# Clip and store of the first tile in one piece instead of three, in a contrast kernel that streams 50 MB through one core

## The chip, the cores and the metric

The kernel runs on one core of a Trainium2 chip. The metric is the device time of one execution in microseconds. Before the change the median of three runs is 239.01 us, the lowest 238.9, the highest 239.16.

## The reference

The input holds 16 pictures of 3 channels, each channel 512 x 512 float32, so 48 images and 50.33 MB; the output has the same size. Each image is stretched around its own mean and clipped:

```
mean = np.mean(x, axis=(2, 3), keepdims=True)
return np.clip(mean + factor * (x - mean), 0, 1).astype(np.float32)
```

With factor f this is clip(f * x + (1 - f) * mean), so a shift per image and then one multiply-add and a clamp per element.

## The kernel before

The whole input is seen as rows of 8192 floats (32 KB, `ROW`), 32 rows to an image. A tile is 128 rows, one on each partition: 4 images, 4 MB. There are 12 tiles. They live in a ring of six slots in on-chip memory (`BUFS = 6`, 32 KB per partition and slot), and every tile is changed in place: it is loaded into its slot, summed, clipped and stored from the same slot.

Four helpers are defined in the kernel function. `load(t, n)` (line 82) issues a load of one tile, or of two in one DMA, from SyncE's queue (SP). `store(t, c0, c1)` (line 85) issues the store of columns c0 to c1 of a tile from ScalarE's queue. `add(t, c0)` makes the sums: ScalarE copies the tile onto itself and accumulates each row (line 96); for tile 0 alone the first 4352 columns are summed by VectorE (line 91) while ScalarE sums the other 3840. A matmul with a constant block matrix (line 100) then adds up the 32 rows of each image, scales by (1 - f) / 262144, and leaves the shift of every partition in PSUM; a float32 matmul is two instructions. `clip(t, c0, c1)` is two VectorE instructions over these columns: multiply by f and add the shift (line 104), then max with 0 and min with 1 (line 112).

The order on each queue is written out by hand. First the loads of tiles 0, 1, 2 and 3 together, and 4 and 5 together are issued. Tile 0 is summed. Then its clip and store are done piece by piece, with the borders given by the module constant `FIRST`:

```
for c0, c1 in zip((0, *FIRST), (*FIRST, ROW)):
    clip(0, c0, c1)
    store(0, c0, c1)
add(1)
```

With `FIRST = (1024, 3072)` the pieces have 1024, 2048 and 5120 columns; that is 4, 8 and 20 KB of each row, and each piece is a DMA of its own (0.5, 1 and 2.5 MB). After that a loop goes over tiles 1 to 11: clip of tile t, sum of tile t + 1, store of tile t (ahead of that sum for t = 1 and 3, behind it otherwise), and the load of tile t + 5. That load goes into the slot of tile t - 1, so SyncE waits before it until tile t - 1 has been stored; the first of these is the load of tile 6, which waits for the store of tile 0. On ScalarE's queue the issue of a store stands between the sums: while it waits for the clip, the sums behind it wait too.

Of the kernel before, what the change touches and what calls it, by code (L numbers as in the profile page):

```python
# [1 line left out]

# [4 lines left out]


P = 128  # L10
ROW = 8192
BUFS = 6
FIRST = (1024, 3072)


@with_exitstack
def kernel(
    ctx: ExitStack,
    tc: tile.TileContext,
    x: bass.AP,  # L20
    factor: float,
    out: bass.AP,
):

    nc = tc.nc
    f32 = mybir.dt.float32
    Alu = mybir.AluOpType
    Act = mybir.ActivationFunctionType  # L30

    B, C, H, W = x.shape
    n_img, n_pix = B * C, H * W
    ppi = n_pix // ROW
    per_tile = P // ppi
    n_tiles = n_img // per_tile
    assert ppi * ROW == n_pix and per_tile * n_tiles == n_img

    factor = float(factor)
    wconst = (1.0 - factor) / float(n_pix)  # L40

    x_f = x.rearrange("b c h w -> (b c h w)")
    out_f = out.rearrange("b c h w -> (b c h w)")

    def dram(ap, t, c0=0, c1=ROW, n=1):
        run = [[P * ROW, n]] if n > 1 else []
        return bass.AP(
            tensor=ap.tensor, offset=t * P * ROW + c0, ap=[[ROW, P], *run, [1, c1 - c0]]
        )

    consts = ctx.enter_context(tc.tile_pool(name="consts", bufs=1))
    xpool = ctx.enter_context(tc.tile_pool(name="xpool", bufs=1))
    small = ctx.enter_context(tc.tile_pool(name="small", bufs=1))
    psum = ctx.enter_context(tc.tile_pool(name="psum", bufs=1, space=bass.MemoryType.PSUM))


    sums = small.tile([P, 2 * n_tiles], f32, name="sums")
    bias = psum.tile([P, n_tiles], f32, name="bias")

    blockw = consts.tile([P, P], f32, name="blockw")  # L60
    blocks = blockw.rearrange("p (a b) -> p a b", b=ppi)
    nc.gpsimd.memset(blockw, wconst)  # L62
    for base, step in ((0, -ppi), (ppi - 1, ppi)):
        nc.gpsimd.affine_select(  # L64
            out=blocks,
            in_=blocks,
            compare_op=Alu.is_ge,
            fill=0.0,
            base=base,
            pattern=[[step, per_tile], [0, ppi]],  # L70
            channel_multiplier=1 if step < 0 else -1,
        )


    ring = xpool.tile([P, BUFS, ROW], f32, name="ring")

    def slots(t, n=1, c0=0, c1=ROW):
        k = t % BUFS
        return ring[:, k, c0:c1] if n == 1 else ring[:, k : k + n, :]

    def load(t, n=1):
        nc.sync.dma_start(out=slots(t, n), in_=dram(x_f, t, n=n))  # L82

    def store(t, c0=0, c1=ROW):
        nc.scalar.dma_start(out=dram(out_f, t, c0, c1), in_=slots(t, 1, c0, c1))  # L85

    def add(t, c0=0):
        own = sums[:, 2 * t : 2 * t + 2]
        parts = []
        if c0:  # L90
            nc.vector.tensor_reduce(  # L91
                out=own[:, 0:1], in_=slots(t, 1, 0, c0), axis=mybir.AxisListType.X, op=Alu.add
            )
            parts.append(own[:, 0:1])
        part = slots(t, 1, c0)
        nc.scalar.activation(out=part, in_=part, func=Act.Copy, accum_out=own[:, 1:2])  # L96
        parts.insert(0, own[:, 1:2])
        shift = bias[:, t : t + 1]
        for k, part in enumerate(parts):
            nc.tensor.matmul(shift, blockw, part, start=k == 0, stop=k == len(parts) - 1)  # L100

    def clip(t, c0=0, c1=ROW):
        part = slots(t, 1, c0, c1)
        nc.vector.tensor_scalar(  # L104
            out=part,
            in0=part,
            scalar1=factor,
            scalar2=bias[:, t : t + 1],
            op0=Alu.mult,
            op1=Alu.add,  # L110
        )
        nc.vector.tensor_scalar(  # L112
            out=part, in0=part, scalar1=0.0, scalar2=1.0, op0=Alu.max, op1=Alu.min
        )

    with tc.manual_schedule():
        load(0)
        load(1)
        load(2, 2)
        load(4, 2)  # L120
        add(0, 4352)
# [4 lines that stand above are left out]
        for t in range(1, n_tiles):  # L126
            clip(t)
            if t in (1, 3):
                store(t)
            if t + 1 < n_tiles:  # L130
                add(t + 1)
            if t not in (1, 3):
                store(t)
            if t + BUFS - 1 < n_tiles:
                load(t + BUFS - 1)


# [1 line left out]
_INS = ['x', 'factor']  # L139
_OUTS = [((16, 3, 512, 512), 'float32')]  # L140

_NUMBERS = {'factor': 1.5}


# [26 lines left out]
```

## Time and profile before

| what | us |
|---|---|
| median of three runs | 239.01 |
| profiled execution, its own time | 238.72 |
| span of the profiled execution | 237.0 |
| VectorE busy | 112.1 |
| ScalarE busy | 82.9 |
| one tile's clip, its two VectorE instructions | 4.49 and 4.43 |
| one tile's sum on ScalarE | 7.03 |

The span goes from the first to the last instruction; some 1.7 us of the profiled execution lie around it. The profile's second part cuts the span in 40 slices and gives the busy share of every engine in tenths, and of the 16 DMA engines together. A stretch of time can be asked for by its ends; its row gives length, then busy time and instructions of TensorE's matmuls and weight loads, VectorE, ScalarE and GpSimd, then TensorE's granted clock, the DMA engines' share, and GB/s. In the timeline a row is start, length, engine, line, operation, tiles; ACTq is the DMA issuing of ScalarE's queue, SPq that of SyncE's. Issuing is merged over neighbouring instructions ("x3" with the time from the first to the end of the last). The packet records of the trace have one entry for each piece that a DMA engine moved: here one row of a tile, and a 4-byte packet with which a DMA reports its end.

### The profile page before, as it was taken

To read this page: it belongs to the slowest core of one execution; us is meant where nothing else is said; L and a number is where in the kernel's file an instruction comes from. 1 tells how busy PE (TensorE), PEld (TensorE's weight loads), DVE (VectorE), ACT (ScalarE), POOL (GpSimd) and SP (SyncE) were. 2 spreads that over 40 slices of the span, in tenths; PEclk is the share of its full clock that TensorE was granted. 3 is DMA by queue.
4 is the path that set the end of the run, shared out by engine and by line. 5 is a ranking of instruction groups with operands and counts; after the bars stand their busy time and mean duration, and the time that the engine had idled before them with its cause. 6 is when DMAs were issued, how large, how long until landed. Compare 5 with 4: busy or idle time off the path is not lost.

```text
span 237.0 us, 211 instructions
## 1 busy us (share of the span) xinstructions
PE 7.6 (3%) x26; PEld 6.5 (3%) x26; DVE 112.1 (47%) x29; ACT 82.9 (35%) x25; POOL 1.0 (0%) x7
## 2 busy tenths in 40 slices
PE   0000000000000000000000000000000000000000
PEld 0000000000000000000000000000000000000000
DVE  0078708609990059979209407704902920950000
ACT  2050190299100894650380091083056029000000
POOL 1000000000000000000000000000000000000000
DMA  7999998999999999999999999999999999999996
GB/s 265 442 442 442 398 459 383 441 428 435 465 426 404 409 442 442 442 442 442 442 426 431 404 420 442 442 442 442 442 442 426 415 398 442 442 442 442 442 442 265
DMA packets 3712, 100.66 MB, mean 425 GB/s; under 512 B 384, under 2 KB 384, under 8 KB 512
## 3 DMA queue, kind: packets, MB, share of 16 engines
q1 hardware_dynamic: 1696, 50.33, 49.6%
q10 hardware_dynamic: 2016, 50.33, 49.2%
HBM read 50.33 MB, written 50.33 MB: 425 GB/s over the span
## 4 chain that ended last, share of the span: by engine, by line
DMA 39%; DVE 25%; another core or an unknown queue 11%; ACT 9%; issue 3%; PE 1%; ACTq 1%; SPq 0%
DMA out_dram<-ring 20%; DMA ring<-in_x_dram 18%; DVE ring L104 11%; DVE ring L112 11%; ACT ring L96 9%; DVE sums L91 2%; PE bias L100 1%; ACTq L85 1%; SPq L82 0%
## 5 line engine op out<-in xcount | busy, mean ns | idle before, releaser
L96 ACT ACTIVATE ring<-ring 128x8192 f32<-128x8192 f32 (+1 forms) x12 | 80.7, 6724 | 117.3 <-DMA ring<-in_x_dram 95.3
L104 DVE TENSOR_SCALAR ring<-ring,bias 128x8192 f32<-128x8192 f32 (+3 forms) x14 | 54.3, 3880 | 84.9 <-PE bias L100 84.9
L112 DVE TENSOR_SCALAR ring<-ring 128x8192 f32<-128x8192 f32 (+3 forms) x14 | 53.4, 3817 | 0.5
L100 PE MATMUL bias<-sums,blockw 128*128 128x1 f32 x26 | 7.6, 361 | 194.0 <-ACT ring L96 193.5
L100 PEld LDWEIGHTS bias<-sums,blockw 128*128 128x128 f32 x26 | 6.5, 312 | 195.0 <-ACT ring L96 177.7
L91 DVE TENSOR_REDUCE sums<-ring 128x1 f32<-128x4352 f32 x1 | 4.7, 4685 | 13.1 <-DMA ring<-in_x_dram 13.1
L96 ACT ACTIVATION_READ_ACCUMULATOR ring<-ring 128x1 f32 x12 | 2.2, 186 | 0.0
L96 ACT ACT_TABLE_LOAD x1 | 1.3, 1283 | 0.8 <-PEq L152 0.8
L64 POOL TENSOR_SCALAR_AFFINE_SELECT blockw<-blockw 128x128 f32<-128x128 f32 x2 | 0.6, 311 | 0.1
L62 POOL MEMSET blockw<- 128x128 f32 x1 | 0.2, 204 | 0.3 <-POOLq L152 0.3
L152 POOL MEMSET const-uint8-127<- 128x1 uint8 x1 | 0.1, 103 | 0.0
L152 POOL MEMSET const-bfloat16-1.0<- 128x1 bf16 x1 | 0.1, 102 | 0.0
L152 POOL MEMSET const-float32-0.0<- 128x1 f32 x1 | 0.1, 98 | 0.3 <-issue 0.3
L152 POOL MEMSET const-float32-1.0<- 128x1 f32 x1 | 0.1, 98 | 0.0
## 6 DMA issues: line engine op xcount, KB each, us to landing
out_dram<-ring ACTq DMA_DIRECT2D x11, 4096.0 KB, 48.5
ring<-in_x_dram SPq DMA_DIRECT2D x8, 4096.0 KB, 31.4
ring<-in_x_dram SPq DMA_DIRECT2D x2, 8192.0 KB, 59.5
out_dram<-ring ACTq DMA_DIRECT2D x1, 2560.0 KB, 37.3
out_dram<-ring ACTq DMA_DIRECT2D x1, 1024.0 KB, 25.8
out_dram<-ring ACTq DMA_DIRECT2D x1, 512.0 KB, 16.1
```

The source lines that it names most:

```text
L62: nc.gpsimd.memset(blockw, wconst)
L64: nc.gpsimd.affine_select(out=blocks, in_=blocks, compare_op=Alu.is_ge, fill=0.0, base=base, pattern=[[step, per_tile], [0, ppi]], channel ...
L85: nc.scalar.dma_start(out=dram(out_f, t, c0, c1), in_=slots(t, 1, c0, c1))
L91: nc.vector.tensor_reduce(out=own[:, 0:1], in_=slots(t, 1, 0, c0), axis=mybir.AxisListType.X, op=Alu.add)
L96: nc.scalar.activation(out=part, in_=part, func=Act.Copy, accum_out=own[:, 1:2])
L100: nc.tensor.matmul(shift, blockw, part, start=k == 0, stop=k == len(parts) - 1)
L104: nc.vector.tensor_scalar(out=part, in0=part, scalar1=factor, scalar2=bias[:, t : t + 1], op0=Alu.mult, op1=Alu.add,)
L112: nc.vector.tensor_scalar(out=part, in0=part, scalar1=0.0, scalar2=1.0, op0=Alu.max, op1=Alu.min)
L152: nc = _bacc.Bacc("TRN2", target_bir_lowering=False, num_devices=1)
```

## The change

The constant that holds the borders is empty. The loop over pieces then runs once, with columns 0 to 8192: tile 0 is clipped by one pair of VectorE instructions over 8192 columns and stored by one DMA of 128 rows of 32 KB, as all other tiles are. Nothing else differs.

```
 ROW = 8192
 BUFS = 6
-FIRST = (1024, 3072)
+FIRST = ()
```

## The prediction

> **What bounds the kernel now.** First the page, parts 1 to 3, for which resource is full; then stretches of time cut at landings, for whether that resource runs at one rate; then the timeline of ScalarE's queue, for when stores are issued; last the trace's records of single DMA packets, for what stands on each of the 16 DMA engines in what order (the records give start, length, size and queue of each packet; from them I only take times).
>
> ```profile
> span 237.0 us, 211 instructions
> PE 7.6 (3%) x26; PEld 6.5 (3%) x26; DVE 112.1 (47%) x29; ACT 82.9 (35%) x25; POOL 1.0 (0%) x7
> DMA  7999998999999999999999999999999999999996
> DMA packets 3712, 100.66 MB, mean 425 GB/s; under 512 B 384, under 2 KB 384, under 8 KB 512
> q1 hardware_dynamic: 1696, 50.33, 49.6%
> q10 hardware_dynamic: 2016, 50.33, 49.2%
> ...
> 12.75:22.43 9.68, 1.15 (x4) 1.00 (x4) 8.57 (x6) 3.50 (x2) 0.00 (x0) 1.00 1.00 433
> 35.77:47.95 12.18, 0.56 (x2) 0.47 (x2) 8.92 (x2) 2.22 (x1) 0.00 (x0) 1.00 1.01 430
> 47.95:65.15 17.20, 1.17 (x4) 1.00 (x4) 11.59 (x3) 11.92 (x4) 0.00 (x0) 1.00 1.00 425
> 84.56:181.38 96.82, 3.52 (x12) 3.01 (x12) 53.42 (x12) 42.65 (x13) 0.00 (x0) 1.00 1.00 434
> ...
> 20.00 8.52 ACTq L85 DMA_DIRECT2D out_dram<-ring  x3
> 28.56 7.03 ACT L96 ACTIVATE ring<-ring 128x8192 f32<-128x8192 f32 x1 [11.96 <-DVE ring L112]
> ...
> 193.87 7.03 ACT L96 ACTIVATE ring<-ring 128x8192 f32<-128x8192 f32 x1 [12.25 <-DMA ring<-in_x_dram]
> 193.93 0.34 ACTq L85 DMA_DIRECT2D out_dram<-ring  x1
> 200.80 0.19 ACT L96 ACTIVATION_READ_ACCUMULATOR ring<-ring 128x1 f32 x1
> 210.65 0.34 ACTq L85 DMA_DIRECT2D out_dram<-ring  x1
> ```
>
> VectorE is at 47%, ScalarE at 35%; the DMA digits are 9 from the second slice to the last but one, and the two queues (q1 loads, q10 stores) together fill 98.8% of the 16 engines' span. The last two columns of a stretch are DMA share and GB/s: pure loads run at 433, loads beside stores of 32 KB rows at 434, and only the two stretches in which the 8 KB and the 20 KB rows of tile 0 are stored are below, at 430 and 425. By the packet records every engine works without a gap from 1.81 (the first engine; 2.45 the last) to 235.83 us. One 32 KB packet takes 1.213 us, and a tile's 8 packets per engine pass in 9.68 us: pure loads land at 12.75 and 22.43, the last stores at 197.11 and 235.83, 4 tiles in 38.72 us. While both queues have work, an engine takes one packet of each in turn, whatever the sizes, and the 9 ns packet that ends a DMA is a turn too. So the end is 24 tiles of packets, plus what is lost to gaps and slow packets; when a store is issued matters only if an engine runs dry.
>
> **The change, part by part.** The sum is made against the profiled execution: 238.72 us, span 237.0, 1.72 around it. It lies 0.29 under the median 239.01 of the runs shown (238.9 to 239.16); I carry the difference over to the median.
>
> VectorE: the six clips of tile 0 (758, 694, 1284, 1226, 2883, 2827 ns, together 9.67 us) become two of 8192 elements (4.49 + 4.43 = 8.92). Clipping starts at 18.48 as before and ends at about 27.45, not 28.10. This is cover only: the DMA engines have loads queued for 6 tiles, 58 us, so it costs and brings nothing.
>
> ScalarE's queue: three issues (20.00, about 22.4, 28.18) become one at 27.45. Behind it the sum of tile 1 starts near 27.8 instead of 28.56, and tile 1's store is issued near 44.6 instead of 45.35. Nothing else stands between on that queue, and SP and POOL aren't passed by anything. If the work on chip were the limit, the gain would be 0.7 us, and the later first store a loss of up to 7.45 us; with the engines full both are 0.
>
> The Trainium skill, DMA: Bandwidth & Descriptors, section Rules for kernel authors, advises to issue a DMA early, so that its setup overlaps compute. The change does the reverse for the first 4 KB of each row; what that would make is the rival of the delay, below, and the gapless packets speak against it here.
>
> DMA work: 256 extra packets go from the store queue, 16 per engine, and two closing packets of 9 ns on each engine. By length the three small rows take 0.159 + 0.309 + 0.761 = 1.229 us against 1.213, times 8 rows per engine 0.13 us. Beside this some 49 loads among the small rows between 35 and 65 us took 1.25 to 1.52 us, on some engines and not on others; among the 32 KB stores from 67 to 236 us none did. What both cost the engine that ends last follows from its landings: 12.75 us for tile 0, then 23 tiles at 9.68 give 235.39, against 235.83 in the trace. So 0.44 us of the span is owed to the small pieces. I take all of it as gained, since the new order of packets is that of 67 to 236 us; at the least the shorter packets alone, 0.06 to 0.13 us, or nothing if the slow loads have another cause. The other end of this term is a loss: if the first 32 KB stores beside loads ran like the stretch of 425 GB/s for two tiles (38.7 us at 2% less), 0.8 us.
>
> When the stores start: the first store now was issued at 20.00 and its first packets started at 24.21 on the first engine, behind three loads, 4.2 us later. Issued at 27.45 it should start at about 31.5, behind 24 loads (1.81 + 24 x 1.21, with the first packet longer by 0.8). Tile 0 then lands at about 51 instead of 65.15, since its large rows take equal turns, and load 6, which waits for it on SP, is issued near 51 instead of 65.57; its queue is full until about 88, so that earlier issue brings nothing. Tiles 2 and 3 land near 51 instead of 44.91 and tiles 4 and 5 near 89 instead of 77.3, as stores take half of the turns; loads end near 204.7 instead of 193.48.
>
> What is late next: a load's landing to the issue of its store takes 193.48 to 210.65, 17.17 us (0.39 to ScalarE, 7.03 + 0.19 sum, 0.6 matmul, 8.92 clip). At the end 25 store packets per engine are left (now 35), 17 of them ahead of the last tile's: 17 x 1.21 = 20.6 us. The engines' stagger of 0.63 us taken off, the last store may need 20.6 - 17.17 - 0.63 = 2.8 us from issue to first packet before an engine runs dry; now it is some 15. The nearest rows for this need are the first load, issued at 0.80, with first packets at 1.81 to 2.45 (1.0 to 1.65), and the first store, 4.2, which stood behind loads already committed. At the end no load is there, so I take 1.0 to 1.65 and cost the edit at 0; with 4.2 the gap would be 1.4 us. The stores of tiles 2 and 4 have similar or more slack, and a late one there costs nothing: a load takes the turn, and that leaves one more store packet, 1.21 us more slack each, for the end.
>
> Sum: 237.0 - 0.44 = 236.56 span, 238.28 with the 1.72, and 239.01 - 0.44 = 238.57, say 238.6, on the median's scale.
>
> **The rivals.**
>
> Slow loads stay: they belong to that time (ScalarE and VectorE both at work in 47.95 to 65.15) and not to the sizes. For it: they fell on only some engines. Against it: 84.56 to 181.38 has the same work beside it at 434. Gain 0.06 to 0.13: 238.9.
>
> The last store comes late (slower): the last tile's path of 17.17 us becomes the end. It decides from a need above 2.8 us between issue and first packet; at the 4.2 of the first store the gap is 1.4, the time 239.01 - 0.44 + 1.4 = 240.0. Against it stands that the same need would first delay the store of tile 2, which has the same 2.8 us, and so add slack.
>
> Large rows hurt the early loads (slower): the 0.8 us above, in place of the gain: up to 239.8. The stretch at 434 speaks against it.
>
> The delay passes through (slower): if the store stream set the end, its later start, 27.45 for 20.00, would move the end by 7.45, to 246.5. Against it: from 24 to 193 us the engines split their turns between both queues without a gap, and loads fill what stores leave.
>
> Each DMA has a fixed price on the engines: the first load was issued at 0.80 and landed at 12.75, 2.27 us more than its 9.68. Two DMAs fewer would then give 4.5 us, 234.5. Against it: four stores end to end took 38.72, just 4 x 9.68, so that price overlaps.
>
> The Trainium skill, same page, section Anatomy of one DMA, puts the fixed part at about 2 us for DMAs issued from GpSimd, mostly the wait for the write's receipt; by it two DMAs fewer would be an estimated 4 us.
>
> **How the numbers follow.** Forecast 0.65; slow loads stay 0.18; late last store 0.09; delay passes through 0.01; large rows hurt 0.05; fixed price 0.02. What can be told from no change is 0.2%, 0.48 us: the border is 238.53, just past the forecast's 238.57, so its 0.65 is split, 0.32 faster and 0.33 same, for the median moves by 0.1 between runs. Adding 0.02 to the first and 0.18 to the second: faster 0.34, same 0.51, slower 0.15. The forecast's own range is 238.2 to 238.9. The whole range goes from 238.1 to 239.4: it takes in the slow loads, a part of the gap and of the hurt, and leaves out the fixed price, the 4.2 us case and the worst of the large rows.
>
> **What would show it.** Packets: 3712 - 256 - 32 = 3424, under 8 KB 352. One ScalarE-queue issue near 27.4. Stretches of 433 to 434 GB/s from 12.75 to the end, no load over 1.25 us after the first. Load 6 issued near 51, loads ending near 204.7, the last store issued near 222 and its packets directly behind those before. Tile 0 landing at 65 would show the turns wrong; a drop in the last slices' DMA digits, a store that came late; a span of 237.0 with all this in place, that slow loads were not the small rows'.

## The result and the profile after

The changed kernel takes 243.03 us, median of six runs (241.21 to 243.27), against 238.95 for the kernel before (238.9 to 239.16). The ratio, of the means, is 1.0157, with a 95% interval of 1.0127 to 1.0186: slower, where the forecast was 238.6 and the range ended at 239.4. The profiled execution took 242.78, with a span of 241.1 us.

The page of the changed kernel, parts 1 to 3:

```profile
span 241.1 us, 200 instructions
PE 7.6 (3%) x26; PEld 6.5 (3%) x26; DVE 111.5 (46%) x25; ACT 82.9 (34%) x25; POOL 1.0 (0%) x7
DMA  7999999999999999999999999999999999999993
DMA packets 3424, 100.66 MB, mean 418 GB/s; under 512 B 352, under 2 KB 352, under 8 KB 352
q1 hardware_dynamic: 1696, 50.33, 49.8%
q10 hardware_dynamic: 1728, 50.33, 48.4%
```

The work is what was forecast: 3424 packets, 352 of them small, and VectorE has 0.6 us less to do. The DMA digits still read 9 from the second slice on, so the engines are no less occupied; only the last digit is 3 in place of 6. The same bytes at 418 GB/s in place of 425 are the loss. The busy share hardly shows it, since packets that take longer count as busy.

Stretches of the changed kernel, about a tile's loads and stores each but for the longer second one (last column GB/s):

```profile
32.50:51.80 19.30, 0.58 (x2) 0.50 (x2) 8.92 (x2) 2.60 (x2) 0.00 (x0) 1.00 1.00 433
52.50:88.20 35.70, 1.18 (x4) 1.01 (x4) 17.75 (x4) 14.13 (x4) 0.00 (x0) 1.00 1.00 432
109.00:128.50 19.50, 0.59 (x2) 0.50 (x2) 15.91 (x4) 7.12 (x2) 0.00 (x0) 1.00 0.99 418
128.50:148.00 19.50, 0.59 (x2) 0.50 (x2) 8.92 (x2) 7.12 (x2) 0.00 (x0) 1.00 0.99 418
148.00:167.50 19.50, 0.58 (x2) 0.50 (x2) 8.92 (x2) 7.12 (x2) 0.00 (x0) 1.00 1.01 425
167.50:187.00 19.50, 0.59 (x2) 0.50 (x2) 8.48 (x2) 7.12 (x2) 0.00 (x0) 1.00 1.00 425
```

The kernel before has these for the same stage:

```profile
103.93:123.29 19.36, 0.58 (x2) 0.50 (x2) 8.92 (x2) 7.11 (x3) 0.00 (x0) 1.00 1.00 433
123.29:142.65 19.36, 0.59 (x2) 0.50 (x2) 8.92 (x2) 7.13 (x3) 0.00 (x0) 1.00 1.00 432
142.65:162.01 19.36, 0.59 (x2) 0.50 (x2) 8.92 (x2) 7.11 (x3) 0.00 (x0) 1.00 1.00 433
```

So the early stage, in which the change was made, runs at 432 to 433 from the first store row on, and most of the loss lies 60 to 150 us later, where both kernels issue the same instructions with the same row sizes. Its place is seen in the packet records. Before, not one 32 KB packet that starts between 90 and 200 us takes over 1.25 us. After, 128 do: 115 loads and 13 stores. They stand at the seam of two tiles, one or more at a seam. This is one DMA engine of the changed kernel at two seams (start, length in us, queue, bytes):

```
109.24 0.009 load 4         129.26 0.009 load 4
109.25 1.321 store 32768    129.26 1.213 store 32768
110.56 1.213 load 32768     130.47 1.213 load 32768
111.77 0.009 store 4        131.68 0.009 store 4
111.78 1.589 load 32768     131.69 2.089 load 32768
113.36 1.213 store 32768    133.78 1.220 store 32768
114.57 1.378 load 32768     134.99 1.213 load 32768
```

A load DMA ends (the 4-byte packet), one store row later the store DMA of the tile three before it ends, and the next load row takes 1.59 or 2.09 us in place of 1.213. In all, 44 of the 115 slow loads come right behind the packet that ends a store DMA and 53 are the second load behind it; each of the 13 slow stores, as the one at 109.25, comes right behind the packet that ends a load DMA. One engine of the kernel before at such a seam, with three store rows between the two ends:

```
115.71 0.009 load 4
115.72 1.213 store 32768
116.93 1.213 load 32768
118.14 1.213 store 32768
119.35 1.213 load 32768
120.56 1.213 store 32768
121.76 1.213 load 32768
122.97 0.009 store 4
122.98 1.213 load 32768
```

Per engine the slow packets of this stage add up to 0.73 to 3.53 us, 1.98 on average. Since the engines differ, they fall apart: the last load ends between 206.35 and 209.51 us (before 193.13 to 193.48), and the last store between 237.3 and 239.76 (before 235.48 to 235.84).

At the end, the timeline of ScalarE's queue after:

```profile
209.89 7.03 ACT L96 ACTIVATE ring<-ring 128x8192 f32<-128x8192 f32 x1 [12.39 <-DMA ring<-in_x_dram]
209.95 0.34 ACTq L85 DMA_DIRECT2D out_dram<-ring  x1
216.83 0.19 ACT L96 ACTIVATION_READ_ACCUMULATOR ring<-ring 128x1 f32 x1
226.67 0.34 ACTq L85 DMA_DIRECT2D out_dram<-ring  x1
```

The sum of the last tile starts when the slowest engine has landed its load, and the store follows 16.78 us later, as before. The fastest engines finish the store ahead of it at 226.93 and stand idle until 227.52, 0.6 us. The slowest finishes it at 230.08 and goes straight on to 239.76. So the idle time is a result of the spread and doesn't set the end.

### The profile page after: what moved, and what is told of

The parts are those of the page before. It is cut to its first block, busy times and chain, and to the rows that moved or that the text cites. A ratio compares the mean times of both kernels' runs of the same rounds, so it can differ in the third digit from the quotient of the medians.

```text
span 241.1 us, 200 instructions
## 1 busy us (share of the span) xinstructions
PE 7.6 (3%) x26; PEld 6.5 (3%) x26; DVE 111.5 (46%) x25; ACT 82.9 (34%) x25; POOL 1.0 (0%) x7
## 2 busy tenths in 40 slices
DMA packets 3424, 100.66 MB, mean 418 GB/s; under 512 B 352, under 2 KB 352, under 8 KB 352
## 4 chain that ended last, share of the span: by engine, by line
another core or an unknown queue 36%; DVE 24%; issue 14%; ACT 12%; DMA 5%; PE 1%; ACTq 1%; DVEq 0%
ACT ring L96 12%; DVE ring L104 11%; DVE ring L112 11%; DMA ring<-in_x_dram 5%; DVE sums L91 2%; PE bias L100 1%; ACTq L85 1%; DVEq L104 0%
## 5 line engine op out<-in xcount | busy, mean ns | idle before, releaser
L104 DVE TENSOR_SCALAR ring<-ring,bias 128x8192 f32<-128x8192 f32 x12 | 53.9, 4490 | 101.6 <-PE bias L100 101.6
L112 DVE TENSOR_SCALAR ring<-ring 128x8192 f32<-128x8192 f32 x12 | 53.1, 4426 | 0.4
```

The lines of the kernel that those rows point to most:

```text
L104: nc.vector.tensor_scalar(out=part, in0=part, scalar1=factor, scalar2=bias[:, t : t + 1], op0=Alu.mult, op1=Alu.add,)
L112: nc.vector.tensor_scalar(out=part, in0=part, scalar1=0.0, scalar2=1.0, op0=Alu.max, op1=Alu.min)
```

## The experiments

What a run has to tell is by how many rows the loads lead the stores. A number that can be read off each engine is N, the store rows that are left when its last load has ended; N modulo 8 (called r here) is how many store rows stand between the end of a load DMA and the end of the next store DMA; on an engine it stays the same from tile to tile. Each trace holds one execution, so N and the slow packets are those of that one; its time is given as "traced" where it lies off the median, and what the others lost isn't shown. Unless said otherwise, slow packets "after 90 us" are counted up to 200 us. Before, N is 35 on all engines, r = 3; after, 25 on 14 engines and 26 on two, r = 1 and 2.

Three theories were set against each other: the phase (r decides), the large first rows (32 KB rows into an empty store queue disturb the engines for good), and the distance (three tiles between loads and stores are too few). Delays were made by clamping values again that are clamped already, ahead of the first store.

**One piece, 3.0 us later.**

```
clip(0, 0, 8192)
again(5440)          # max 0, min 1 over columns 0 to 5440
store(0, 0, 8192)
```

> One piece, and VectorE clamps the first 5440 columns of tile 0 a second time before its store is issued (about 3.0 us, values unchanged). The store stream starts about 3 rows later: when the loads end, 27 to 28 store rows are left instead of 25. Theory of the phase (loads are slow where a load DMA and a store DMA end within a row or two of each other on an engine; now they are three rows apart, as before the change): the slow loads at every tile from 92 to 195 us go, the 0.9 us at the first store stays, 239.5 to 240.2 us. Theory of the large first rows (the first store of 32 KB rows sets the engines apart and that goes on): 242.5 to 243.5. Theory of the distance (stores three tiles behind the loads disturb them, four tiles don't): 242.5 to 243.5. If only the delay counted: 246.

Measured: 240.57 us (239.85 to 241.01; traced 239.85), ratio 1.0068 [1.0051, 1.0085]; N is 27 on 13 engines and 26 on three. One packet after 90 us is slow instead of 128. A delay took 2.5 us off the time. The large first rows are out as the cause of the late loss, and so is the distance of about three tiles. The median lies a little above the range of the phase.

**One piece, 8.9 us later**: `again(8192)` twice.

> One piece, and VectorE clamps the whole of tile 0 twice more before its store is issued (about 8.9 us, values unchanged). The store stream starts 7 to 8 rows later: 32 to 33 store rows are left when the loads end, so DMA ends fall together as after the change, at four tiles' distance. Theory of the phase: slow loads at every tile as after the change, 242 to 243.5 us. Theory of the large first rows: 242.5 to 243.5. Theory of the distance: 239.5 to 240.

Measured: 239.62 us, ratio 1.0028 [1.0019, 1.0038], no slow packet after 90 us. The expectation had put the bad phase at r = 0; N came out as 31 on 15 engines and 32 on one, and neither is bad. The time fits the distance, which the run before had ruled out. So the theory of the phase as it was written here failed, and what was left was that r = 1, perhaps 2, is the bad phase.

**Two pieces**: `FIRST = (1024,)`.

> Two pieces, of 1024 and 7168 columns (rows of 4 and 28 KB). The first store starts as before the change, so 27 store rows are left when the loads end. Theory of the phase: three rows apart, no slow loads per tile, 238.4 to 239.2 us. Theory of the large first rows: as before the change, 238.8 to 239.3, if 4 KB first is what protects. Theory of the distance: three tiles' distance, 242 to 243.

Measured: 239.24 us, ratio 1.0016 [1.0002, 1.003]; N is 27 on 12 engines and 26 on four, no slow packet after 90 us. It rules out the distance once more. It lies just above the phase's range and inside that of the large first rows, so it doesn't tell these two apart.

**The kernel before with its first store 7.1 us later**: `again(1024)` ten times after the first piece.

> The kernel before, with ten further clamps of the first 1024 columns (about 7.1 us, values unchanged) ahead of the first store. The store stream starts 6 rows later: about 41 store rows are left when the loads end instead of 35, DMA ends within a row of each other, at five tiles' distance. Theory of the phase: slow loads at every tile, 241 to 243 us though the first rows are small. Theory of the large first rows, and of the distance: as before, 238.8 to 239.3.

Measured: 239.25 us (238.84 to 240.57, four of ten above 240; traced 238.98), ratio 1.0021 [1.0003, 1.004], no slow packet after 90 us. It told nothing apart: N was 37 and not 41, since the load queue ran empty for a few rows, waiting for the store of tile 0. The bad phase was not reached.

**All stores ahead of the sums, in the changed kernel.** This tests a further theory, that the slow loads come from a store being issued just at the seam.

```
-            if t in (1, 3):
+            if True:
                 store(t)
             if t + 1 < n_tiles:
                 add(t + 1)
-            if t not in (1, 3):
+            if False:
                 store(t)
```

> The changed kernel with every store issued ahead of the next tile's sum, so at the end of its clip and not when the next load has landed (in the changed kernel's trace the stores of tiles 6 to 10 are issued at 130.3, 150.4, 170.7, 190.4 and 209.95, just as the engines pass from one tile to the next). The order of packets stays, 25 rows are left at the end of the loads. Theory of the issue (slow loads come from a store being issued while the engines are at the seam of two tiles): no slow loads after 92 us, 239.5 to 240. Theory of the phase (load DMAs and store DMAs end within a row or two of each other): 242.5 to 243.3 as without this edit.

Measured: 242.74 us, ratio 1.0155 [1.0138, 1.0172], 126 slow packets after 90 us. When the store is issued doesn't matter.

**One piece, 10.7 us later**: `again(8192)` twice and `again(3072)`.

> One piece, and about 10.7 us of further clamps of tile 0 ahead of its store (values unchanged). About 33 rows are left when the loads end: the same phase as after the change, one row after the load's end, but eight rows further back. Theory of the phase: slow loads at each tile, 241.5 to 243.5. Theory of the distance (the stores are too close behind the loads, about three tiles): no slow loads at the tiles, 239.4 to 240.

Measured: 242.28 us, ratio 1.0139 [1.0122, 1.0156]; N is 33 on 15 engines, r = 1. The ratio is of three executions, 242.18 to 242.32. The traced one was far longer (251.55 us) because of a single engine that no longer agrees with the others: with N = 32 it had 11.7 us of slow packets after 90 us and ended at 248.55, the others by 237.7. On those others the slow packets came to 0.46 to 1.6 us. Eight rows more of distance and the same r give about the same time as after the change, as the phase had it, and 1.8 us less delay (the run with 8.9) takes the loss away.

**Tiles 2 to 5 loaded one by one, in the changed kernel.** Each 4-byte packet that ends a DMA is a turn of its queue, so two more load DMAs let the stores catch up.

```
-        load(2, 2)
-        load(4, 2)
+        load(2)
+        load(3)
+        load(4)
+        load(5)
```

> The changed kernel with tiles 2, 3, 4 and 5 loaded by a DMA each. Two more packets that end a load take a turn, so stores gain one row: 24 left instead of 25, and load and store DMAs end in neighbouring turns. Tile 2 also lands 5 to 10 us earlier, so its store is early. Theory of the phase: slow loads at the tiles as after the change or worse, 242 to 244. Theory of the distance: the same. Theory of the issue: 242 to 243. If 24 rows are free of it, it is the one row between the ends that matters, 239.5 to 240.

Measured: 239.78 us, ratio 1.0033 [1.0023, 1.0044]; N is 23 on 13 engines and 24 on three. No slow packet after 90 us but a few store rows at the very end. With no delay, and one or two rows nearer than the changed kernel, the slowdown is gone, against the expectation of the phase as it was written here (242 to 244). On three engines the packet that ends a store DMA follows directly behind the one that ends a load DMA; on 13 the store DMA ends one load row and one store row ahead of the load DMA, the mirror image of the changed kernel. So two ends close together do no harm by themselves.

**One piece, 1.8 us later**: `again(3136)`.

> One piece, and about 1.8 us of further clamps ahead of the store of tile 0. About 26 rows are left. In the run with 3.0 us, four engines with 26 rows left had no slow loads at the tiles. Theory of the phase on each engine by itself: 239.5 to 240.5, no slow loads. Theory of a resource that the engines share, where most of them must be in the bad phase: with most engines at 26, either none, 239.5 to 240.5, or about as after the change, 242 to 243, if two rows are still too near.

Measured: 242.07 us (240.76 to 242.19), ratio 1.0119 [1.0093, 1.0146]. The 11 engines at N = 26 have 0.08 us of slow packets after 90 us on average, the five at 25 have 1.09 (0.5 to 2.65). One of these ended at 239.19 and set the time; the others ended by 237.5. So within one run the engines part by their r, and one engine is enough to make a run slow. But each engine by itself isn't the whole of it: the two engines of the changed kernel at r = 2 (N = 26), beside 14 at r = 1, lost 2.7 and 2.8 us, and those at r = 2 here next to nothing. This trace also has 26 slow loads between 60 and 90 us, 0.5 us per engine, most of them at 72 to 76 where the store of tile 2, issued at 69.31, comes in; the changed kernel has none between 60 and 90. (The run with 3.0 us had three engines at 26, not four.)

**The crossing: the kernel before, with tiles 2 to 5 loaded one by one.** The edit to the loads is the one shown above for the changed kernel, on the other kernel.

> The kernel before, three pieces, with tiles 2 to 5 loaded by a DMA each. Two more packets that end a load take a turn after the first store has started, so the stores gain two rows on the loads: 33 left when the loads end instead of 35, one row after the end of a load DMA. Theory of the phase (slow loads where a store DMA ends one or two rows after a load DMA): slow loads at each tile, 241.5 to 243 us, though the three pieces are kept and nothing else is changed. Theory of the pieces (the small first rows are what protects): 238.8 to 239.3.

Measured: 250.76 us (248.91 to 252.5; traced 252.5), ratio 1.0491 [1.043, 1.0552]. r is 1 on 15 engines and 0 on one, and 141 packets after 90 us are slow. The page of this kernel:

```profile
span 250.8 us, 212 instructions
DMA  7999999999999999999999999999999999997900
```

The two zeros at the end are one engine at work and 15 that have finished: 15 ended by 238.8 us, and one at 249.44, the one with r = 0. On that engine 37 of the 45 store rows between 73 and 195 us took 1.29 to 1.86 us, anywhere in a tile, and only two of the 45 loads were slow. That is not the picture of slow loads at the seams, and the theory of the phase doesn't hold it: it expected 241.5 to 243, about what the other 15 engines would give (238.8 and the 3.1 us that lay between the last store's end and the time in the kernel before, 241.9). The edit that took 3.3 us from the changed kernel adds 11.8 to the one before, some 10 of them by this one engine.

**The same edit with two pieces.**

> Two pieces of 1024 and 7168 columns, with tiles 2 to 5 loaded by a DMA each. 25 rows left instead of 27, the phase of the changed kernel. Theory of the phase: 241.5 to 243.5 us, against 239.24 for the two pieces with the paired loads. Theory of the pieces: 239 to 239.5.

Measured: 243.05, 251.32, 251.79 and 254.24 us, too far apart for a ratio; the profiled execution is the shortest, with N = 25 on all engines as far as their packets can be followed, 133 slow packets after 90 us, and a span of 241.3. That one lies in the range of the phase; the others, at least 8 us longer, have no trace. Two pieces alone took 239.24.

**The kernel before, with only tiles 2 and 3 loaded one by one.**

> The kernel before with only tiles 2 and 3 loaded by a DMA each. One row less: 34 left, two rows after the end of a load DMA, as most engines in the run with 1.8 us of delay. Theory of the phase: slow loads, 240.5 to 242.5. Theory of the pieces: 238.8 to 239.3.

Measured: 240.39 us, ratio 1.0063 [1.0046, 1.008] (traced 239.9), just under the phase's range. Two engines are at N = 33 and have 0.79 and 0.85 us of slow packets after 90 us, all stores right behind the end of a load DMA; the other 14, at 34, have none. These two ended at 236.9, the others by 236.2.

**One piece, 5.4 us later**: `again(8192)` and `again(1536)`, to see what the one piece costs when no engine is near the bad phase.

> One piece, and about 5.4 us of further clamps of tile 0 ahead of its store (values unchanged), so that 29 to 30 rows are left when the loads end: a store DMA ends five or six rows after a load DMA, far from the bad phase on every engine, where the run with 3.0 us still had engines at 26 and 27. Theory of the phase: no slow loads after 60 us, only the 0.8 us at the first store that all kernels show and little else, 239.0 to 239.6, so that one piece by itself costs 0.0 to 0.3%. Theory of the large first rows: over 241.

Measured: 239.34 us, ratio 1.0019 [1.0009, 1.0028]; N is 28 and 29, one slow packet after 90 us.

```profile
span 237.8 us, 203 instructions
DMA  7999999999999999999999999999999999999996
```

So of the 1.57% some 1.4 are the phase and 0.2 the one piece itself, if the delay of 5.4 us costs nothing of its own. The latter is seen at the first store: between 20 and 60 us the slow loads add 0.87 us per engine after the change (loads 23 and 24, just ahead of the first store row, took up to 2.7 us), 0.82 in this run, 0.41 before.

Taken together: engines with r of 3 to 7 have next to no slow packets after 90 us in any run, at 23 to 37 rows left; engines with r = 1 have them in every run, with one, two or three pieces, at 25 and at 33 rows; engines with r = 2 have none or few where most others keep clear of 1 (the runs with 3.0 and 1.8 us of delay, two pieces, tiles 2 and 3 apart), but 0.4 to 2.8 us where most are at 1 (the changed kernel, and it with stores first). At r = 0 three engines of one run and one of another had none, in runs without an engine at 1; one ran away with 11.7 us, and the one that ran away in the crossing is at 0 too, both beside 15 engines at 1. So r = 1 is the bad phase, and engines at 0 and 2 suffer where most others are at 1: that suggests something shared between the engines, which no run here isolates. None of the versions beats the kernel before.

## Why the prediction was wrong

**That failed:** "when a store is issued matters only if an engine runs dry", and with it "I take all of it as gained, since the new order of packets is that of 67 to 236 us". The new order is one load, one store in turn, as there, but with the streams 25 rows apart and not 35, and that decides at each seam what a load takes. The working had both numbers (25 and 35 rows left), and used them only for the slack at the end. The term of the sum was -0.44 us; the phase put in its place 1.98 us per engine on average and up to 3.5, and the engines that lose most set the end. The engine that ended last lost 3.25 us at the seams and 1.5 at the first store.

**The size of the first term was wrong too, and its sign.** The 0.44 us were laid to the small rows. But slow loads come with the start of the store stream whatever its rows, and there are more of them with larger rows: 0.41 us per engine with 4, 8 and 20 KB rows, 0.74 with 4 and 28, 0.87 with 32. (The moment seems to count as well: the small rows 7.1 us later had 0.62.) So the rival "slow loads stay" was right that they don't go, and the rival "large rows hurt the early loads" that they grow; with the phase out of the way one piece is 0.41 us slower (239.34 against 238.93), not 0.44 faster.

**Right:** that the engines work nearly without a gap and the clip's 0.7 us and the store's later issue cost nothing by themselves; runs with the store 3 to 9 us later still are faster than the changed kernel. Right also the packet counts, the first store row behind 24 loads (32.5 us on the first engine, forecast 31.5), tile 0 landing at 51.8 to 52.5 (51) and load 6 issued at 53.13 (51). The alternation with a turn for each closing packet stands in the records, and the experiments on loads rest on it.

**The rivals:** the late last store came true in part, 0.6 us of idle time on the fast engines, but on engines that don't set the end. Its forecast stagger of 0.63 us was 3.16, which used up the 2.8 us of slack. From its issue to its first packets took 0.85 us there, less than the 1.0 to 1.65 taken. The rival on large rows took its 0.8 us from the stretch at 425 GB/s; beside the large rows the changed kernel ran at 432 to 433, and the early loss, about half of that price, lay in the two loads ahead of the first store row. That the run ended above this rival's 239.8 was the phase, which no rival held. The delay that passes through and the fixed price per DMA did not show.

**What stays open** is what makes a load slow where a store DMA ends one row behind a load DMA. The Trainium skill, DMA: Bandwidth & Descriptors, section Queues, rings and completion order, says that a DMA's closing write lands only after every earlier write of that engine, across its queues; a wait of that kind would fit a slow packet just behind a seam. That the slow stores come right behind the end of a load DMA, and 44 of the slow loads right behind the end of a store DMA, fits as well. But the changed kernel with single loads has the two ends next to each other on three engines, and one row apart in the other order on 13, and no slow load, so nearness alone isn't it. Open too is whether the engines share something, and why an engine at r = 0 can run away on its stores. A run that moves the closing packets and leaves the rows as they are would tell more; it was not tried.

## What to carry to other kernels

Where two DMA queues share full engines in turns, the number of rows by which one leads the other is a setting of the kernel: it is fixed by the moment at which the second stream starts and by how many DMAs either stream is cut into, and it holds to the end. Read it off the packet records, compare the landing of one DMA over the engines, and look for packets over the usual length at the seams, since the busy share shows next to nothing of this. A kernel that runs well at one lead can lose 1 to 5% by an edit that moves it two rows (two pieces, from 27 to 25 rows, and the kernel before, from 35 to 33), in a stage that the edit doesn't touch, so an edit to the start of a stream is to be judged at several leads.

## What the runs showed of the hardware

A 32 KB row takes an engine 1.213 us, load or store, and a closing packet of 4 bytes 9 ns, but that packet uses up a turn. A store row that stands behind loads in full engines starts 4.2 us (before) to 4.9 us (after) after its issue. Slow loads at a bad seam took 1.25 to 2.2 us, and one engine, at r = 0 beside 15 at 1, took 10 us longer than the others for the same work: 249.44 against 238.8 at the latest.
